# A two-layer hybrid attention kernel: five chunks of 512 columns in place of seven of 256 and 384

## The chip, the cores and the metric

The kernel runs on one core of one Trainium2 chip. The metric is the device time of one execution in microseconds; the times shown are the median of three runs and their spread. One further execution was recorded by the hardware profiler, and all rows below come from that one.

## The reference

There are two layers over 256 tokens with a model width of 1024, all in float32. In each layer the input is normed and multiplied by `w_in` (1024 x 3584) into ten groups of columns: queries, keys, values and gate of a block attention (`aq ak av ag`, 6 heads of 64, so 384 columns each), the same four of a dilated attention (`bq bk bv bg`, 384 each), and queries and gate of an attention over 256 rows of memory (`mq mg`, 4 heads, 256 each). Memory's keys and values come from the normed memory times `w_mem_kv` (1024 x 512). Queries and keys are normed per head and, but for memory's, rotated by position.

```python
a_q, a_k, a_v, a_g, b_q, b_k, b_v, b_g, m_q, m_g = jnp.split(proj, cuts, axis=-1)
qa = rope(rms_norm(to_heads(a_q, N_HEADS_MOBA), qk_g[0]))
mkv = jnp.einsum('bmd,de->bme', rms_norm(mem, mem_norm_g), w_mem_kv)
km = rms_norm(to_heads(m_k, N_HEADS_MEM), qk_g[5])
y = jnp.concatenate([oa * jax.nn.silu(a_g), ob * jax.nn.silu(b_g), om * jax.nn.silu(m_g)], axis=-1)
return x + jnp.einsum('bte,ed->btd', y, w_out)
```

At 256 tokens the block attention is one causal block, and the three dilated patterns are one attention whose mask holds the logarithm of how many patterns allow a pair.

## The kernel before, in words

**Products.** Each float32 matrix product is made of three products of a rounded format: weights and inputs are split into a high and a low half (`hi`, `lo` in L430 and L431; `xmh`, `xml` in L183 and L186), and `products` (L146) issues high x high, low x high and high x low. Only the first two of memory's eight blocks of rows go through whole, in full float32 (`WHOLE`).

**Projections.** `project` (L216) computes one chunk of n columns for both halves of the tokens: two accumulator banks, eight blocks of 128 rows, three products, so 48 matmuls of n columns. `project_t` (L235) computes the gates transposed, with 256 columns to a matmul. The order of the chunks is `order` (L371): memory's keys and values (`mkv`, 512 columns), `mq` 256, `mg`, `bq`, `bk`, `bv` 384 each, the gate in two parts, `aq`, `ak`, `av` 384 each, the gate, and then the rows of `w_out` for the three attentions. There are four accumulator banks (`acc`), three work banks (`wk`) and one for the outputs of a pair of heads.

**Weights.** `loads` (L389) brings units of up to 1 MB into three raw buffers by DMA, nearly all on SP's queue (the very first unit on ScalarE's), each as soon as a raw buffer is free. `split` (L419) makes the high half on ScalarE and the low half on VectorE, four splits ahead of their use.

**Order.** Every TensorE instruction is kept in the order in which the program was written out (`pe`, L103). That order is made by a small planner: `clock` adds up the time of the matmuls, and the attention of a pair of heads is a generator whose steps (turn queries and keys, scores, turn the probabilities, outputs) come due some microseconds of that clock later (`D_NORM`, `D_QK`, ... in L32) and are put between two steps of the projection that is then under way (`poll`, L125). The other engines run in program order where `pin` (L90) says so, which is the case up to the end of the first layer's first projections; behind it, the instructions are ordered by priority, which is program order where nothing else is said. An accumulator tile takes a bank that is free when the compiler's scheduler comes to it.

**Norms.** `normed` (L257) squares an accumulator on ScalarE, sums by head on VectorE, takes a power on GpSimd, and multiplies by one table (memory) or by two for the rotation, four or six VectorE instructions in all. `start_heads` (L546) starts the pairs of heads of a group when the norms of its queries and keys are issued: for `b` behind `bk`, for `a` behind `ak`, all three pairs at once.

**Start of the first layer.** `gT` holds the gains of the input norms and comes by GpSimd's queue. Memory's keys and values are projected from the unnormed rows; the factors of its norm (`rmem`) come later from the squares of `mem_sb` (L561 to L567) and scale the evicted tile `kv` (L572). Memory's keys are normed behind memory's queries (L570 to L573).

## Time and profile before

| | |
|---|---|
| median of 3 runs | 295.46 us (295.03 to 296.15) |
| the profiled execution | 295.58 us |
| its span, first to last instruction | 293.8 us |
| mean granted TensorE clock | 1.000 |
| TensorE matmul busy | 285.1 us, 97% |
| VectorE busy | 204.5 us, 70% |
| ScalarE busy | 200.1 us, 68% |
| GpSimd busy | 56.0 us, 19% |
| DMA | 47.33 MB, mean 161 GB/s |

Busy times come from single instructions; those of TensorE overlap, so that a start-to-start spacing is read from the timeline. In the rows, L is the line of the kernel, `out<-in` are the program's names, a form such as `128x384` is partitions x elements, and what stands in brackets is the idle time of the engine before that row and what ended it.

### The profile page before, as it was taken

To read this page: it belongs to the slowest core of one execution; us is meant where nothing else is said; L and a number is where in the kernel's file an instruction comes from. 1 tells how busy PE (TensorE), PEld (TensorE's weight loads), DVE (VectorE), ACT (ScalarE), POOL (GpSimd) and SP (SyncE) were. 2 spreads that over 40 slices of the span, in tenths; PEclk is the share of its full clock that TensorE was granted. 3 is DMA by queue.
4 is the path that set the end of the run, shared out by engine and by line. 5 is a ranking of instruction groups with operands and counts; after the bars stand their busy time and mean duration, and the time that the engine had idled before them with its cause. 6 is when DMAs were issued, how large, how long until landed. Compare 5 with 4: busy or idle time off the path is not lost.

```text
span 293.8 us, 4977 instructions
## 1 busy us (share of the span) xinstructions
PE 285.1 (97%) x1810; PEld 250.2 (85%) x1810; DVE 204.5 (70%) x456; ACT 200.1 (68%) x445; POOL 56.0 (19%) x74
## 2 busy tenths in 40 slices
PE   7799999999999999999999999999999999999994
PEld 5489989698998999877788999989899899987773
DVE  1588899887656997654485668879655699765413
ACT  2799968795888646987364654868588864698600
POOL 1003598030001230000011049703000123000000
PEclk9999999999999999999999999999999999999999
DMA  7999656327347248246207726560823715820003
GB/s 231 378 366 355 208 143 229 78 102 220 106 113 240 62 158 310 98 166 207 80 8 243 222 101 174 189 172 9 274 60 108 240 47 170 304 99 29 3 0 143
DMA packets 32681, 47.33 MB, mean 161 GB/s; under 512 B 1152, under 2 KB 27536, under 8 KB 32656
## 3 DMA queue, kind: packets, MB, share of 16 engines
q1 hardware_dynamic: 32048, 45.95, 48.4%
q10 hardware_dynamic: 576, 1.05, 1.0%
q8 instruction: 14, 0.23, 0.3%
q14 instruction: 11, 0.09, 0.1%
q0 software_dynamic: 32, 0.02, 0.0%
HBM read 45.96 MB, written 1.05 MB: 160 GB/s over the span
## 4 chain that ended last, share of the span: by engine, by line
PE 81%; DVE 6%; DMA 5%; ACT 3%; issue 2%; POOL 1%; SPq 0%; DVEq 0%; ACTq 0%
PE acc L111 64%; PE wk L114 7%; PE o L111 5%; PE wk L111 5%; DMA raw<-in_w_in_dram 3%; DMA memT<-in_mem_t_dram 2%; DVE lo L431 2%; DVE xml L186 1%; ACT hi L430 1%; POOL hrs L156 1%; DVE hss L263 1%; ACT xmh L183 1%; POOL r L156 0%; DVE ms L155 0%; ACT pr L334 0%
## 5 line engine op out<-in xcount | busy, mean ns | idle before, releaser
L431 DVE TENSOR_TENSOR lo<-raw,hi 128x768 fp32r<-128x768 f32 (+1 forms) x91 | 97.2, 1091 | 31.0 <-ACT hi L430 30.9
L430 ACT CAST hi<-raw 128x768 fp32r<-128x768 f32 (+1 forms) x91 | 83.8, 937 | 33.0 <-PE acc L111 24.4
L111 PE MATMUL acc<-hi,xmh 128*128 128x384 f32 (+2 forms) x252 | 67.0, 348 | 1.7 <-ACT hi L430 1.7
L111 PE MATMUL acc<-hi,xml 128*128 128x384 f32 (+2 forms) x252 | 63.6, 335 | 0.0
L111 PE MATMUL acc<-lo,xmh 128*128 128x384 f32 (+2 forms) x252 | 63.5, 335 | 0.0
L156 POOL TENSOR_TENSOR hrs<-ms,mhalf 128x6 f32<-128x6 f32 (+1 forms) x24 | 30.3, 1264 | 118.9 <-DVE ms L155 118.5
L111 PEld LDWEIGHTS acc<-hi,xmh 128*128 128x128 f32 x252 | 42.6, 189 | 7.1 <-issue 3.0
L111 PEld LDWEIGHTS acc<-lo,xmh 128*128 128x128 f32 x252 | 45.0, 188 | 1.2
L111 PEld LDWEIGHTS acc<-hi,xml 128*128 128x128 f32 x252 | 44.9, 188 | 1.2
L111 PE MATMUL acc<-hi,yT 128*128 128x512 f32 x128 | 41.0, 402 | 0.0
L111 PE MATMUL acc<-xmh,hi 128*128 128x256 f32 x128 | 29.7, 293 | 0.0
L341 ACT ACTIVATE pr<-pr,nm 128x128 f32<-128x128 f32 (+1 forms) x48 | 21.4, 446 | 12.0 <-DVE nm L339 11.8
L111 PE MATMUL acc<-xmh,lo 128*128 128x256 f32 x128 | 28.4, 283 | 0.0
L111 PE MATMUL acc<-xml,hi 128*128 128x256 f32 x128 | 28.3, 282 | 0.0
L111 PEld LDWEIGHTS acc<-hi,yT 128*128 128x128 f32 x128 | 23.0, 188 | 4.9 <-issue 0.7
L347 ACT ACTIVATE pr<-pr,rinv 128x128 f32<-128x128 f32 (+1 forms) x64 | 25.6, 462 | 0.0
L111 PE MATMUL acc<-lo,yT 128*128 128x512 f32 x64 | 25.0, 391 | 0.0
L111 PEld LDWEIGHTS acc<-xmh,hi 128*128 128x128 f32 x128 | 20.9, 191 | 0.7 <-issue 0.7
L111 PEld LDWEIGHTS acc<-xml,hi 128*128 128x128 f32 x128 | 21.0, 191 | 0.0
L111 PEld LDWEIGHTS acc<-xmh,lo 128*128 128x128 f32 x128 | 21.0, 191 | 0.0
L358 ACT COPY pT<-wk 128x384 f32<-128x384 f32 (+1 forms) x32 | 15.5, 506 | 6.8 <-PE wk L114 6.8
L339 DVE CUSTOM_DVE_ANT_0 pr<-wk,cst 128x128 f32<-128x128 f32 (+1 forms) x48 | 14.3, 354 | 5.3 <-PE wk L111 5.3
(77 smaller groups left out, 356.8 us busy)
## 6 DMA issues: line engine op xcount, KB each, us to landing
raw<-in_w_in_dram SPq DMA_DIRECT2D x24, 768.0 KB, 4.9
raw<-in_w_in_dram SPq DMA_DIRECT2D x7, 1024.0 KB, 5.3
raw<-in_w_out_dram SPq DMA_DIRECT2D x6, 1024.0 KB, 6.1
raw<-in_w_in_dram SPq DMA_DIRECT2D x6, 512.0 KB, 3.7
raw<-in_w_out_dram SPq DMA_DIRECT2D x4, 512.0 KB, 4.3
raw<-in_w_mem_kv_dram SPq DMA_DIRECT2D x2, 1024.0 KB, 5.2
raw<-in_w_mem_kv_dram ACTq DMA_DIRECT2D x4, 256.0 KB, 5.4
raw<-in_w_mem_kv_dram SPq DMA_DIRECT2D x2, 512.0 KB, 7.5
```

The source lines that it names most:

```text
L111: pe(nc.tensor.matmul(out, a, b, start=start, stop=stop), us)
L114: pe(nc.tensor.transpose(out, a, ident), 0.109)
L156: pin(nc.gpsimd.tensor_tensor(dst, ms, mhalf[:, :n], op=ALU.pow))
L183: pin(nc.scalar.activation(hi[:, k], v[:, a], AF.Copy, scale=g[:, k:k + 1]))
L186: pin(nc.vector.scalar_tensor_tensor(lo[:, k], v[:, a], g[:, k:k + 1], hi[:, k].bitcast(F32), op0=ALU.mult, op1=ALU.subtract))
L263: pin(nc.vector.tensor_reduce(ss, heads(sq), axis=AX.X, op=ALU.add))
L339: nc.vector.tensor_tensor_reduce(out=pr[:, spans[t]], in0=s[:, spans[t]], in1=masks[t], scale=-1.0, scalar=3e38, op0=ALU.add, op1=ALU.min, ...
L341: nc.scalar.activation(pr[:, spans[t]], pr[:, spans[t]], AF.Exp, scale=-1.0, bias=nm[:, t:t + 1], accum_out=sums[:, t:t + 1])
L347: nc.scalar.activation(pr[:, spans[t]], pr[:, spans[t]], AF.Copy, scale=rinv[:, t:t + 1])
L358: nc.scalar.copy(pT[:, :n], ps[:, :n])
L430: pin(nc.scalar.copy(hi, raw))
L431: pin(nc.vector.tensor_tensor(lo, raw, hi.bitcast(F32), op=ALU.subtract))
```

## The change

Queries, keys and values of a layer are projected in five chunks of 512 columns, put together from pieces of the column groups:

| chunk | columns |
|---|---|
| c0 | all of `mq`, `bv` 128 to 384 |
| c1 | all of `bq`, `bk` 0 to 128 (one piece in memory) |
| c2 | `bk` 128 to 384, `aq` 0 to 128, `bv` 0 to 128 |
| c3 | `aq` 128 to 384, `ak` 0 to 256 (one piece) |
| c4 | `ak` 256 to 384, all of `av` (one piece) |

The gate chunks and `w_out` stay. A unit of a mixed chunk is loaded with one DMA for each piece. `normed` is divided into `inverse_norms` (square, sum, power) and `normed` (the tables), which takes ranges of columns with a table for each. Queries and keys of a group share a tile `qk` of 768 columns.

Pairs of heads start in parts: the first pair of `b` behind c1, the other two behind c2; the first two of `a` behind c3, the last behind c4. `D_NORM` goes from 8 to 11. The norms, the softmax, the copies of turned tiles and the output products are issued with a priority 60 instructions earlier (`urgent`). In the first layer the squares of memory's rows, the scalings of `kv` and the norm of memory's keys are issued inside c0, and the constants' DMA earlier; the norm of memory's queries follows c0. The second layer's split of memory (`next_mem`) is started with `a` instead of `b`. `gT` is loaded on SP's queue behind the first block of memory, the fourth piece of the first weight unit on SP's queue, and `mem_sb` shares the buffer of the first weight unit.

```diff
-D_NORM, D_MEM, D_QK, D_SOFTMAX, D_PT, D_EVAC = 8, 1, 2.5, 5, 2.5, 4
+D_NORM, D_MEM, D_QK, D_SOFTMAX, D_PT, D_EVAC = 11, 1, 2.5, 5, 2.5, 4
+URGENT = 60
...
-    tc.keep_in_program_order(nc.gpsimd.dma_start(gT, gains))
...
+    def urgent():
+        return tc.high_priority(offset=URGENT)
...
+    def inverse_norms(acc):
+        n = acc.shape[-1]
+        with urgent():
+            sq = sp.tile([P, n], F32, tag="sq", name="sq", bufs=2)
+            pin(nc.scalar.activation(sq, acc, AF.Square))
...
+            rsqrt(rs, ss, n // HD, 1.0 / HD)
+        return rs
+    def normed(acc, rs, dst, tables):
+        n = acc.shape[-1]
+        with urgent():
+            t1 = sp.tile([P, n], F32, tag="t1", name="t1", bufs=2)
+            for lo, hi, tab in tables:
+                pin(nc.vector.tensor_tensor(heads(t1[:, lo:hi]), heads(acc[:, lo:hi]),
+                                            tab[0][:, None, :].to_broadcast([P, (hi - lo) // HD, HD]), op=ALU.mult))
...
-            step = 1 if u == 0 else 2 if u == 1 else 4 if u == 2 else nk
+            step = 1 if u == 0 else 2 if u == 1 else nk
...
-                queue = nc.scalar if u == 0 else nc.sync
+                queue = nc.scalar if u == 0 and b < 3 else nc.sync
...
+        if k == 0:
+            pin(nc.sync.dma_start(gT, gains))
...
-        mq, steps = project(xs, weights(), 256)
+        mq, steps = project(xs, weights(), 512)
...
-            if i == 3 and l == 0:
-                mem_junk = sp.tile([P, D], F32, tag="v", name="mem_junk", bufs=2)
+            if i == 1 and l == 0:
+                mem_junk = sp.tile([P, D], F32, tag="tab", name="mem_junk", bufs=1)
                 r_mem.append(row_scale(mem_sb, 0, "rmem", mem_junk))
+                pin(nc.sync.dma_start(cst, const))
+                load_gains(0, 4)
+            if i == 2 and l == 0:
+                r_mem.append(row_scale(mem_sb, 1, "rmem", mem_junk))
+                pin(nc.scalar.activation(kv[:, 0], kv[:, 0], AF.Copy, scale=r_mem[0]))
+            if i == 3:
+                if l == 0:
+                    pin(nc.scalar.activation(kv[:, 1], kv[:, 1], AF.Copy, scale=r_mem[1]))
+                for t in range(NT):
+                    normed(kn[:, t], inverse_norms(kn[:, t]), kn[:, t], [(0, 256, [gB[:, l, 5]])])
         for t, acc in enumerate(mq):
-            normed(acc, 256, qn[:, t], [gB[:, l, 4]])
...
+            normed(acc[:, 0:256], inverse_norms(acc[:, 0:256]), qn[:, t], [(0, 256, [gB[:, l, 4]])])
+            pin(nc.scalar.copy(v_b[:, t, 128:384], acc[:, 256:512]))
...
-            if l + 1 < DEPTH and kind == 2:
+            if l + 1 < DEPTH and kind == 0:
...
+                for t, acc in enumerate(run(project(xs, weights(), 512))):
+                    normed(acc, inverse_norms(acc), qk[:, t, 0:512], [(0, 384, table(2, t)), (384, 512, table(3, t))])
+                start_heads(range(1), e0, qn, kn, masks, v, gate, ready)
+                for t, acc in enumerate(run(project(xs, weights(), 512))):
+                    rs = inverse_norms(acc[:, 0:384])
+                    normed(acc[:, 0:256], rs[:, 0:4], qk[:, t, 512:768], [(0, 256, table(3, t))])
+                    nc.scalar.copy(v[:, t, 0:128], acc[:, 384:512])
+                    normed(acc[:, 256:384], rs[:, 4:6], qk_a[:, t, 0:128], [(0, 128, table(0, t))])
+                start_heads(range(1, 3), e0, qn, kn, masks, v, gate, ready)
```

## Rows read from the trace of the kernel before

**Rows 1.** The page's part 1: busy us, share of the span, instructions.

```profile
PE 285.1 (97%) x1810; PEld 250.2 (85%) x1810; DVE 204.5 (70%) x456; ACT 200.1 (68%) x445; POOL 56.0 (19%) x74
```

**Rows 2.** The waits of TensorE, longest first: us in total, times, longest us.

```profile
PE acc L111 <- ACT hi L430: 1.7, 1, 1.7
```

**Rows 3.** Timeline of TensorE: start us, us, what, count, idle before and its releaser.

```profile
1.04 3.35 PE L121 MATMUL warm<-blank 128*128 128x128 f32 x14 [1.04 <-DVE mhalf L83]
...
10.97 1.20 PE L111 MATMUL acc<-hi,xmh 128*128 128x512 f32 x4 [1.72 <-ACT hi L430]
...
13.84 1.07 PE L111 MATMUL acc<-hi,xmh 128*128 128x512 f32 x4
14.74 1.07 PE L111 MATMUL acc<-hi,xml 128*128 128x512 f32 x4
...
21.07 0.40 PE L111 MATMUL acc<-hi,xmh 128*128 128x256 f32 x2
...
32.34 0.40 PE L111 MATMUL acc<-xmh,lo 128*128 128x256 f32 x2
...
38.73 0.33 PE L114 MATMUL wk<-ident,kn 128*128 128x128 f32 x1 [0.46 <-DVE kn L277]
...
52.02 0.70 PE L111 MATMUL wk<-qkT 64*128 64x256 f32 x2
53.19 1.13 PE L111 MATMUL wk<-qkT 64*128 64x256 f32 x6 [0.48 <-ACT pT L358]
54.25 0.62 PE L111 MATMUL acc<-hi,xmh 128*128 128x384 f32 x2
```

**Rows 4.** The chain that ended last, in order of time: start us, us, what.

```profile
19.07 8.12 DMA raw<-in_w_in_dram
...
60.94 0.87 PE wk L114 x8
61.82 4.17 PE acc L111 x24
...
193.09 1.06 PE wk L111 x8
```

**Rows 5.** Groups of instructions by shape: busy us, mean ns of one, idle before.

```profile
L431 DVE TENSOR_TENSOR lo<-raw,hi 128x1024 fp32r<-128x1024 f32 x43 | 51.6, 1219 | 14.4 <-ACT hi L430 14.4
...
L431 DVE TENSOR_TENSOR lo<-raw,hi 128x768 fp32r<-128x768 f32 x48 | 45.8, 976 | 16.6 <-ACT hi L430 16.5
...
L532 DVE SCALAR_TENSOR_TENSOR gate<-th,acc 128x256 f32<-128x256 f32 x16 | 6.2, 415 | 4.1 <-ACT th L531 3.9
...
L531 ACT ACTIVATE th<-acc 128x256 f32<-128x256 f32 x16 | 5.4, 375 | 0.6 <-PE acc L111 0.6
```

**Rows 6.** Timeline of ScalarE, 22 to 30 us.

```profile
22.61 2.04 ACT L430 CAST hi<-raw 128x1024 fp32r<-128x1024 f32 x2
...
25.46 1.13 ACT L161 ACTIVATE mem_junk<-mem_sb 128x1024 f32<-128x1024 f32 x1
...
27.26 0.83 ACT L430 CAST hi<-raw 128x768 fp32r<-128x768 f32 x1 [0.58 <-DMA raw<-in_w_in_dram]
...
29.58 0.72 ACT L572 ACTIVATE v<-v,rmem 128x512 f32<-128x512 f32 x1
```

**Rows 7.** Two stretches: busy us of PE, PEld, DVE, ACT, POOL; clock, DMA, GB/s.

```profile
14.00:21.00 7.00, 7.00 (x40) 6.01 (x40) 5.63 (x12) 6.16 (x11) 1.13 (x2) 1.00 1.09 360
60.00:70.00 10.00, 10.00 (x72) 9.19 (x71) 10.00 (x19) 8.10 (x14) 2.65 (x2) 1.00 0.29 78
```

**Rows 8.** Timeline of VectorE, 29 to 32 us.

```profile
29.01 0.41 DVE L263 TENSOR_REDUCE hss<-sq 128x4 f32<-128x256 f32 x1
...
31.10 0.41 DVE L263 TENSOR_REDUCE hss<-sq 128x4 f32<-128x256 f32 x1
...
31.62 0.42 DVE L267 TENSOR_TENSOR t<-acc,gB 128x256 f32<-128x256 f32 x1
```

**Rows 9.** Timeline of GpSimd, 29 to 31 us.

```profile
29.70 1.02 POOL L156 TENSOR_TENSOR hrs<-ms,mhalf 128x4 f32<-128x4 f32 x1 [2.05 <-DVE ms L155]
```

More of the change, by code (lines that the diff above doesn't have):

```diff
@@ L287, in pair_of_heads @@
         qkT = sp.tile([P, 2, T], F32, tag="qkT", name="qkT", bufs=SLOTS)
-        nc.scalar.copy(qkT.rearrange("p c t -> p (c t)"), ps)
+        with urgent():
+            nc.scalar.copy(qkT.rearrange("p c t -> p (c t)"), ps)
         me = live["pairs"]
@@ L321, in pair_of_heads @@
         y = sp.tile([P, T], F32, tag="y", name="y", bufs=2)
-        nc.vector.scalar_tensor_tensor(y, o, 0.5, gate[:, pair], op0=ALU.mult, op1=ALU.mult)
+        with urgent():
+            nc.vector.scalar_tensor_tensor(y, o, 0.5, gate[:, pair], op0=ALU.mult, op1=ALU.mult)
         live["o"] -= 1
@@ L372, in hybrid_kernel @@
     for l in range(DEPTH):
-        order += [(l, c) for c in ["mkv", "mq", "mg", "bq", "bk", "bv", "bg0", "bg1", "aq", "ak", "av", "ag0", "ag1", "om", "ob", "oa"]]
+        order += [(l, c) for c in ["mkv", "c0", "mg", "c1", "c2", "bg0", "bg1", "c3", "c4", "ag0", "ag1", "om", "ob", "oa"]]
     units = []
@@ L379, in hybrid_kernel @@
         else:
-            n = 512 if c == "mkv" else in_cols[c][1]
+            n = 512 if c == "mkv" else sum(hi - lo for lo, hi in in_cols[c])
             nk = 8 if n <= 256 else 4
@@ L464, in hybrid_kernel @@
     load(RAW_BUFS + 1)
+    mem_sb = sp.tile([P, NT, D], F32, tag="yT0", name="mem_sb", bufs=1)
     pin(nc.sync.dma_start(mem_sb, mem.rearrange("(t p) c -> p t c", p=P)))
@@ L542, in finished @@
             done.add(e)
-            nc.scalar.copy(yT[0][:, e], y)
-            nc.vector.tensor_tensor(yT[1][:, e], y, yT[0][:, e].bitcast(F32), op=ALU.subtract)
+            with urgent():
+                nc.scalar.copy(yT[0][:, e], y)
+                nc.vector.tensor_tensor(yT[1][:, e], y, yT[0][:, e].bitcast(F32), op=ALU.subtract)
         def start_heads(pairs, e0, qn, kn, masks, v, gate, ready, delay=D_NORM):
-            for pair in range(pairs):
+            for i, pair in enumerate(pairs):
                 spawn(pair_of_heads(qn, kn, pair, masks, v, gate, ready,
-                                    lambda y, e=e0 + pair: finished(y, e)), delay + D_PAIR * pair)
-        qn, kn, kv, gate = head_tiles(256, 512)
-        v = kv[:, :, 256:512]
+                                    lambda y, e=e0 + pair: finished(y, e)), delay + D_PAIR * i)
+        kv, gate = head_tiles(512, 256)
+        kn, v = kv[:, :, 0:256], kv[:, :, 256:512]
+        qn = sp.tile([P, NT, 256], F32, tag="mqn", name="mqn", bufs=1)
+        v_b, gate_b = head_tiles(384, 384)
         ready = dict(gate=1e9)
-        mq, steps = project(xs, weights(), 256)
+        mq, steps = project(xs, weights(), 512)
         for i, _ in enumerate(steps):
@@ L584, in hybrid_kernel @@
                 masks = [cst[:, C_CAUSAL + 128:C_CAUSAL + 256], cst[:, C_CAUSAL:C_CAUSAL + 256]]
-            if l + 1 < DEPTH and kind == 2:
+            if l + 1 < DEPTH and kind == 0:
                 mem_xs = xm_tiles()
                 spawn(next_mem(mem_xs, gT[:, 24 + 8 * l:32 + 8 * l]), D_FIRST_MEM)
-            qn, kn, v, gate = head_tiles(384, 384)
             ready = dict(v=1e9, gate=1e9)
-            for i, dst in ((0, qn), (1, kn)):
-                for t, acc in enumerate(run(project(xs, weights(), 384))):
-                    normed(acc, 384, dst[:, t], (tab[:, kind + i, 0, t], tab[:, kind + i, 1, t]))
@@ L593, in hybrid_kernel @@
-            start_heads(3, e0, qn, kn, masks, v, gate, ready)
-            for t, acc in enumerate(run(project(xs, weights(), 384))):
-                nc.scalar.copy(v[:, t], acc)
+            if kind == 2:
+                v, gate, qk, qk_a = v_b, gate_b, queries_and_keys(), queries_and_keys()
+                qn, kn = qk[:, :, 0:384], qk[:, :, 384:768]
+                for t, acc in enumerate(run(project(xs, weights(), 512))):
[7 more added lines that the diff above has]
+                start_heads(range(1, 3), e0, qn, kn, masks, v, gate, ready)
+            else:
+                (v, gate), qk = head_tiles(384, 384), qk_a
+                qn, kn = qk[:, :, 0:384], qk[:, :, 384:768]
+                for t, acc in enumerate(run(project(xs, weights(), 512))):
+                    normed(acc, inverse_norms(acc), qk[:, t, 128:640],
+                           [(0, 256, table(0, t)), (256, 512, table(1, t))])
+                start_heads(range(2), e0, qn, kn, masks, v, gate, ready)
+                for t, acc in enumerate(run(project(xs, weights(), 512))):
+                    normed(acc[:, 0:128], inverse_norms(acc[:, 0:128]), qk[:, t, 640:768], [(0, 128, table(1, t))])
+                    nc.scalar.copy(v[:, t], acc[:, 128:512])
+                start_heads(range(2, 3), e0, qn, kn, masks, v, gate, ready)
```

121 lines of the change are left out of this document (55 added, 66 removed), and 4 rows, old and new, of the table in_cols.

## The prediction

> **What bounds the kernel now.** I read the busy shares first. TensorE's matmul row is busy 97% of the span, VectorE 70% [rows 1]. A busy matmul row only says that some matmul was in flight, so the next view is the list of waits with TensorE alone: its largest entry is one wait of 1.7 us near the start [rows 2]. Then the timeline, to see at what spacing the matmuls start, since durations overlap. Matmuls over 512 columns start four per 0.90 us (13.84 to 14.74), 226.7 ns each to the precision of a longer run; those over 256 columns are 48 + 48 from 21.07 to 32.34, 94 spacings of 119.9 ns [rows 3]. Over 384 columns the chain of waits shows a pure run of 24 in 4.17 us, 173.6 ns [rows 4]. So the middle of the kernel is one stream of matmuls back to back, and a matmul costs its columns over 2.4 GHz plus about 13.3 ns: 106.7 + 13.2, 160 + 13.6, 213.3 + 13.4. The reader is to see two things: the stream has hardly a hole outside the start, and its price per matmul is known at all three widths.
>
> The holes that are left lie in the first layer. At 38.73 TensorE has waited 0.46 us for normed memory keys. At 52.02 the scores of the second memory pair begin, stop after two of eight matmuls, and the next matmul of a projection comes at 54.25: 2.23 us [rows 3] where eight such matmuls take 1.06 us elsewhere [rows 4], so 1.17 us lost behind a ScalarE copy that frees a work bank.
>
> **The change part by part.** *Five chunks of 512.* Per layer the queries', keys' and values' projections were 48 matmuls of 256 columns and 6 x 48 of 384: 48 x 119.9 + 288 x 173.6 = 5.76 + 50.00 = 55.75 us. Now they are 5 x 48 of 512: 240 x 226.7 = 54.41 us. The columns are the same 122,880; what goes is the fixed part of 96 matmuls, 1.3 us a layer, **2.6 us** for both. It lies on the stream that sets the end, so it counts in full.
>
> The Trainium skill, "TensorE: Matmul & The Clock Gate", section "Back-to-back issue gap", speaks against this part: there the isolated spacing at the full clock is the columns over 2.4 GHz plus 2.5 ns. By that, 96 matmuls fewer are worth 0.24 us a layer and 0.5 us in all. This trace doesn't agree: the remainder is 13 ns at each of three widths [rows 3, 4], and the sum keeps 2.6 us.
>
> *Splits and norms.* Per layer, 2 splits of 1024 and 24 of 768 elements become 20 of 1024: on VectorE 20 x 1.219 against 2 x 1.219 + 24 x 0.976, 1.5 us less [rows 5]. The norms go the other way: 64 VectorE instructions a layer become 80, since a chunk that holds queries and keys multiplies by two tables. From the two split sizes an instruction's fixed part is at most 0.25 us, so up to 4 us more. Off the path while the stream's weights are split a chunk ahead; if that cover went, it would be paid in the windows after the two big norms, where VectorE is already full (below). Moving the next layer's memory split to the second group empties ScalarE and VectorE in the first layer's busiest stretch.
>
> *TensorE later behind a norm (8 to 11 us), norms and softmax ahead of later work.* The waits at 38.73 and 52.02 go: the memory pairs are turned at 12 us behind the first chunk instead of 9, and the copy that blocked the scores now ranks ahead of the splits beside it. Gain 0 to 1.6 us; I take **1.6**, since both waits were for work that stood behind splits.
>
> *Gains vector and the fourth weight piece move to SP's queue.* The first matmuls wait for a gain vector, but what follows waits for the memory block and the weights' high half until 10.97 [rows 3], so only that restart counts. One quarter of the first weight leaves ScalarE's queue and goes behind that block: between 0 and 0.8 us earlier, and then the second half of the normed input, which nothing here hurries, holds the stream again. I take 0.2 us. The extra DMAs (two to three for each unit of a mixed chunk) are issues on SP, which waits for buffers most of the time.
>
> *Memory's keys normed inside the first chunk.* This is the step that can cost. In the first layer all of it is pinned in program order. After the first chunk's second step ScalarE must take, in this order: the high half of the memory gate's weights, the square of memory row 0, the second high half, the square of row 1, the scaling of the values' first half, the high half of the next chunk, the second scaling; only then the squares of the keys, and behind them those of the queries. The first of these waits for its DMA. Before, that transfer (768 KB) ran from 19.07 to 27.19 [rows 4], and ScalarE waited for it [rows 6]. Now it is 1 MB; at about 360 GB/s [rows 7] 256 KB more are 0.7 us: 27.9. Then three high halves at 1.0, two squares at 1.1, two scalings at 0.65 [rows 6]: 6.5 us, and the first keys' square is done at about 34.8. VectorE does four norms in strict order, 2.09 us each (reduction at 29.01, the next at 31.10) because each waits for a power on GpSimd of 1.02 [rows 8, 9]; before, the queries came first, now the keys. The queries' banks are read for the last time 0.94 us into the third and the fourth norm (31.62 + 0.42 - 31.10): 34.8 + 4.2 + 0.9 = 39.9 and 42.0.
>
> TensorE's side: the first chunk starts at 21.07 and takes 48 x 0.2267 = 10.9 us, the memory gate 48 x 0.12 = 5.8: it reaches the next chunk at 37.7. There are four accumulator banks; two hold the queries, two the memory gate. The new chunk needs two at once. The gate's banks come free after a tanh of 0.38 and a product of 0.42 each [rows 5], some 38.6 and 39.3, if VectorE lets the products in between its norms. So the stall is 1.6 us with the gate's banks, 2.2 with one of each, 4.3 with the queries' two, and nothing only if ScalarE is not held as I reckon. Queued behind the waiting matmul is all of TensorE's order. I take **2.2**, the middle case. In the second layer nothing waits for memory's rows, and the keys are normed half a chunk before the queries.
>
> **Sum**, on the profiled execution (295.58 us, span 293.8 and 1.8 around it; 0.12 above the median of the runs): -2.6 - 1.6 - 0.2 + 2.2 = -2.2 us. On the median of 295.46 that is **293.3 us**.
>
> **The rivals.** *The stall at the second chunk is not there* (ScalarE reaches the norms earlier, or the gate's banks come free at once): -2.6 - 1.6 - 0.2 = -4.4, 291.1 us. For it: before, the queries' norm was off the path. Against it: ScalarE did wait for that DMA, and the order is fixed.
>
> *The stall is whole*: the new chunk gets the queries' own banks and waits for the fourth norm. -4.4 + 4.3: 295.4 us, no change. For it: before, in this place the new chunk did follow the queries' banks and found them read (31.62 + 0.42) just half a microsecond before it began. Against it: with the keys first, the gate's banks are free sooner.
>
> *Slower: the whole stall and then a slow clock.* The granted clock is 1.00 in every stretch shown [rows 7], but the 14 warm-up matmuls, the first after idleness, ran at 0.22 us apiece (13 spacings in 3.35 less one duration of 0.42) [rows 3], where 128-column transposes take 0.109 (0.87 for eight) [rows 4]: half the rate, the 1.2 GHz level. The Trainium skill, "TensorE: Matmul & The Clock Gate", in its table "Why this matters for your kernels", warns of idle gaps between bursts of matmuls for this reason; no gap in this trace behind the warm-up is long enough to show it. If TensorE idles some 4 us and restarts at half rate for as long as the warm-up lasted, it loses half of 3.4 us or, over twice that time, 3.4: -4.4 + 4.3 + 1.7 to 3.4 = +1.6 to +3.3, 297.1 to 298.8 us. It decides from a stall at which the granted clock falls below 1.00; with one bank free in the middle of the wait a matmul breaks the gap, which speaks against it.
>
> **How the numbers follow.** Half a per cent is 1.5 us, about what this kernel's runs (295.03 to 296.15) can tell from none. Chances: the middle stall 0.43 (its own range 292.3 to 294.6), no stall 0.22, the whole stall 0.22, slower 0.13, into which I also put VectorE falling behind: it is busy 10.00 of 10 us in 60 to 70 [rows 7], there without holding TensorE. Faster by over 0.5% (under 294.0): all of no stall and about four fifths of the middle, 0.56. Slower by over 0.5% (over 296.9): 0.13. Within: 0.31. The range leaves out a tenth at each end: 291.0, just under no stall, to 296.6, between the whole stall and the slow clock.
>
> **What would show it.** Right: 240 matmuls of 512 columns a layer 0.227 us apart; no wait at the memory pairs' scores; TensorE's longest wait, 1.5 to 2.5 us, before the first matmul of the chunk behind the memory gate at about 38 us, released by VectorE; ScalarE waiting for the gate's weights until about 28. Wrong: a spacing at 512 columns clearly above 0.227 us, a gap over 1 us in the second layer, a granted clock under 1.00, or waits of TensorE for low halves behind the norms of the 512-column chunks, which would mean that VectorE has become the bound.

## The result and the profile after

The changed kernel takes **308.27 us** (median of 4 runs, 307.18 to 309.68) against 295.68 on the same chip: 1.0435 times as long, 95% interval 1.0408 to 1.0462. The forecast was 293.3 us, in a range of 291.0 to 296.6; the kernel is 12.6 us slower than before and far outside the range.

The page of the changed kernel, part 1 and two rows of part 2 (40 slices of 7.7 us), stands against [rows 1]:

```profile
PE 289.6 (94%) x1618; PEld 230.4 (75%) x1618; DVE 205.4 (67%) x476; ACT 199.4 (65%) x437; POOL 56.1 (18%) x73
...
PE   8999849999899999989999999999989999989994
...
PEclk9999968999999999999999999999999999999999
```

192 matmuls fewer, and VectorE and ScalarE as busy as before in microseconds. No engine got work that would explain 12 us, so TensorE must stand still or run slower. Part 2 shows both: slices at 8 or less, and a clock row that dips in the sixth and seventh slice. The list of TensorE's waits (us in total, times, longest) names what it stands for; before, the longest wait was 1.7 us [rows 2]:

```profile
PE acc L114 <- DVE ms L158: 5.3, 1, 5.3
PE wk L117 <- ACT pr L363: 2.4, 4, 0.7
PE wk L117 <- DVE nm L355: 2.4, 2, 1.2
...
PE wk L117 <- ACT pT L375: 0.7, 2, 0.4
...
```

**The wait ahead of the second chunk.** TensorE's timeline of the changed kernel at its start and at the first matmul of c1 (start, us, then the row's name; in brackets the idle time before and what ended it), against [rows 3]:

```profile
10.03 1.20 PE L114 MATMUL acc<-hi,xmh 128*128 128x512 f32 x4 [0.58 <-ACT hi L451]
...
36.62 0.40 PE L114 MATMUL acc<-xmh,lo 128*128 128x256 f32 x2
42.36 1.51 PE L114 MATMUL acc<-hi,xmh 128*128 128x512 f32 x2 [5.34 <-DVE ms L158]
43.66 1.05 PE L114 MATMUL acc<-hi,xml 128*128 128x512 f32 x2
...
47.08 1.01 PE L114 MATMUL acc<-lo,xmh 128*128 128x512 f32 x2
...
48.39 0.62 PE L114 MATMUL acc<-hi,xml 128*128 128x512 f32 x2
...
49.75 0.62 PE L114 MATMUL acc<-hi,xml 128*128 128x512 f32 x2
```

5.34 us without a matmul, and behind it pairs of matmuls 0.86 us apart (43.66 to 47.08: 3.42 for eight) instead of 0.453 (48.39 to 49.75: 1.36 for six). The windows of the changed kernel (stretch, its us, busy us of PE, PEld, DVE, ACT and POOL, then the granted clock, the DMA share and GB/s) give half the clock, the 1.2 GHz level, over 41 to 48 us.

```profile
36.00:41.00 5.00, 1.02 (x9) 0.81 (x7) 4.06 (x10) 4.58 (x8) 2.24 (x2) 1.00 0.53 149
41.00:48.00 7.00, 5.64 (x13) 4.16 (x14) 5.74 (x14) 1.34 (x3) 2.37 (x3) 0.51 0.74 219
48.00:55.00 7.00, 7.00 (x35) 5.79 (x34) 3.38 (x4) 3.22 (x5) 6.88 (x16) 1.00 0.48 152
```

Why 5.34? The list names `ms`, which ended last before the restart (at 42.29), but VectorE's product for the gate (`gate`, done at 42.21) is what frees a bank. ScalarE first, to compare with [rows 6], then VectorE over the wait, to compare with [rows 8], both of the changed kernel:

```profile
29.12 1.05 ACT L451 CAST hi<-raw 128x1024 fp32r<-128x1024 f32 x1 [3.45 <-DMA raw<-in_w_in_dram]
...
35.29 0.71 ACT L265 ACTIVATE sq<-v 128x256 f32<-128x256 f32 x2
...
37.12 0.63 ACT L555 ACTIVATE th<-acc 128x256 f32<-128x256 f32 x2
...
42.65 0.37 ACT L607 COPY v<-acc 128x256 f32<-128x256 f32 x1 [2.07 <-DVE t L278]
```

```profile
38.13 0.41 DVE L267 TENSOR_REDUCE hss<-sq 128x4 f32<-128x256 f32 x1
38.46 1.22 DVE L452 TENSOR_TENSOR lo<-raw,hi 128x1024 fp32r<-128x1024 f32 x1
...
40.00 1.22 DVE L452 TENSOR_TENSOR lo<-raw,hi 128x1024 fp32r<-128x1024 f32 x1
41.14 0.41 DVE L289 TENSOR_TENSOR v<-t,hrs 128x256 f32<-128x256 f32 x1
41.47 0.41 DVE L267 TENSOR_REDUCE hss<-sq 128x4 f32<-128x256 f32 x1
41.80 0.41 DVE L556 SCALAR_TENSOR_TENSOR gate<-th,acc 128x256 f32<-128x256 f32 x1
```

c1 got one bank of memory's gate and the queries' first one. The gate's tanh is done at 37.75 (37.12 + 0.63), but the product that frees its bank starts at 41.80: VectorE takes it in its order behind the second norm of memory's keys and two low halves of c1's own weights, which are needed only once c1 runs. The queries' bank costs another 0.49 us: c1's second matmul, at 43.07, waits for ScalarE's copy of the values out of that bank (42.65 to 43.02), and not for the gate's second product. The size of the wait is that of one execution: in the profiles of the runs 3, 8, 11 and 12 below, whose program is the same up to here, it was 3.9 to 5.0 us.

**Late attention, in both layers.** To turn a tile is to transpose it by a product with the unit matrix (`wk<-ident`); the softmax of a pair of `a` or `b` begins when VectorE adds the masks to its scores (`pr<-wk,cst`). The first pair of `b` and the last of `a` show it, in TensorE's and VectorE's timeline of the changed kernel:

```profile
75.66 1.02 PE L114 MATMUL wk<-qkT 64*128 64x128 f32 x8
...
83.84 0.84 PE L117 MATMUL wk<-ident,pr 128*128 128x128 f32 x3 [0.73 <-ACT pr L363]
...
129.04 0.93 PE L114 MATMUL wk<-qkT 64*128 64x128 f32 x8
130.31 0.66 PE L117 MATMUL wk<-ident,qk 128*128 128x128 f32 x4 [0.34 <-ACT pT L375]
132.15 0.55 PE L117 MATMUL wk<-ident,pr 128*128 128x128 f32 x3 [1.18 <-DVE nm L355]
```

```profile
73.37 0.42 DVE L278 TENSOR_TENSOR t<-acc,tab 128x256 f32<-128x256 f32 x1 [2.29 <-ACT sq L265]
...
80.67 0.43 DVE L289 TENSOR_TENSOR qk<-t,hrs 128x256 f32<-128x256 f32 x1 [0.82 <-POOL hrs L159]
...
81.22 0.28 DVE L355 CUSTOM_DVE_ANT_0 pr<-wk,cst 128x128 f32<-128x128 f32 x1
...
128.97 2.36 DVE L452 TENSOR_TENSOR lo<-raw,hi 128x1024 fp32r<-128x1024 f32 x2 [0.45 <-ACT hi L451]
131.25 0.28 DVE L355 CUSTOM_DVE_ANT_0 pr<-wk,cst 128x128 f32<-128x128 f32 x1
```

The scores begin at 75.66; VectorE reads them first at 81.22, 5.6 us later, when c2's norms (73.37 to 81.1) are through, and TensorE stands at 83 for the probabilities. The last pair of `a` has its queries turned at 130.31 between another pair's scores and its softmax, on the third work bank, while the masks stand behind two low halves. Against the usual spacing of each kind of matmul these holes (64, 82.8, 129.6, 207, 226, 273) sum to some 7.6 us, good to half a microsecond.

**The account** on the profiled executions (308.51 against 295.58, +12.9): wait ahead of c1 5.3 + 0.5; half clock 2.7 (first experiment); late attention 7.6; against it the packing 2.6, the two old waits 1.6, the start 0.9 (10.97 to 10.03). That is +11.0, and 1.9 us are left. Most of them, 1.6 us, are three smaller delays in each layer behind the same probabilities (0.2 to 0.3 us each, at 84.2 to 85.5 and 227.7 to 228.9). The start is no gain of its own: what TensorE is early, it waits longer ahead of c1. In the third run it restarts at 10.72, and that wait is 3.9 us.

### The profile page after: what moved, and what is told of

Read it like the earlier page. It is cut to its first block, busy times and chain, and to the rows that moved or that the text cites. A ratio compares the mean times of both kernels' runs of the same rounds, so it can differ in the third digit from the quotient of the medians.

```text
span 306.7 us, 4622 instructions
## 1 busy us (share of the span) xinstructions
PE 289.6 (94%) x1618; PEld 230.4 (75%) x1618; DVE 205.4 (67%) x476; ACT 199.4 (65%) x437; POOL 56.1 (18%) x73
## 4 chain that ended last, share of the span: by engine, by line
PE 59%; ACT 15%; DVE 11%; DMA 7%; issue 5%; POOL 2%; POOLq 0%; SPq 0%; DVEq 0%; ACTq 0%
PE acc L114 48%; PE wk L117 5%; DVE lo L452 4%; DMA raw<-in_w_in_dram 3%; ACT pr L363 3%; ACT hi L451 3%; PE o L114 3%; ACT pr L357 2%; PE wk L114 2%; DMA x_sb<-in_x_dram 2%; ACT pr L350 2%; POOL hrs L159 2%; DVE t L278 1%; DVE hss L267 1%; DMA raw<-in_w_mem_kv_dram 1%
## 5 line engine op out<-in xcount | busy, mean ns | idle before, releaser
L452 DVE TENSOR_TENSOR lo<-raw,hi 128x1024 fp32r<-128x1024 f32 x79 | 96.1, 1226 | 44.9 <-ACT hi L451 44.9
L451 ACT CAST hi<-raw 128x1024 fp32r<-128x1024 f32 x79 | 81.9, 1050 | 43.6 <-PE acc L114 31.3
L114 PE MATMUL acc<-hi,xmh 128*128 128x512 f32 x188 | 61.7, 415 | 5.9 <-DVE ms L158 5.3
L114 PE MATMUL acc<-hi,xml 128*128 128x512 f32 x188 | 58.1, 397 | 0.0
L114 PE MATMUL acc<-lo,xmh 128*128 128x512 f32 x188 | 57.8, 395 | 0.0
L159 POOL TENSOR_TENSOR hrs<-ms,mhalf 128x4 f32<-128x4 f32 (+3 forms) x24 | 31.2, 1300 | 140.5 <-DVE ms L158 140.5
L114 PEld LDWEIGHTS acc<-hi,xmh 128*128 128x128 f32 x188 | 33.2, 192 | 14.0 <-issue 7.5
L363 ACT ACTIVATE pr<-pr,rinv 128x256 f32<-128x256 f32 (+1 forms) x64 | 25.1, 462 | 0.0
L117 PE MATMUL wk<-ident,pr 128*128 128x128 f32 x104 | 18.1, 284 | 5.4 <-ACT pr L363 2.4
L117 PEld LDWEIGHTS wk<-ident,pr 128*128 128x128 f32 x104 | 11.9, 140 | 12.8 <-ACT pr L363 5.8
```

The costliest lines, as they stand in the source:

```text
L114: pe(nc.tensor.matmul(out, a, b, start=start, stop=stop), us)
L117: pe(nc.tensor.transpose(out, a, ident), 0.109)
L159: pin(nc.gpsimd.tensor_tensor(dst, ms, mhalf[:, :n], op=ALU.pow))
L363: nc.scalar.activation(pr[:, spans[t]], pr[:, spans[t]], AF.Copy, scale=rinv[:, t:t + 1])
L451: pin(nc.scalar.copy(hi, raw))
L452: pin(nc.vector.tensor_tensor(lo, raw, hi.bitcast(F32), op=ALU.subtract))
```

## The experiments

All are edits of the changed kernel (of 308.27 us); ratios are to the kernel before.

**1. Keep TensorE at work during the wait.** 26 products of the unit matrix go between the gate and c1 in the first layer.

```
+        if l == 0:
+            filler = o_p.tile([P, T], F32, tag="o", name="filler")
+            for _ in range(26):
+                pe(nc.tensor.matmul(filler[:, 0:P], ident, ident, start=True, stop=True), 0)
```

> The changed kernel with 26 idle matmuls of 128 columns (52 records of 0.109 us, 5.7 us) put on TensorE between the first layer's memory gate and the next chunk, where it stands still for 5.5 us. Theory A (the stand-still lets the granted clock fall to half, and half a clock from 41.1 to 47.9 us costs the matmuls of 42.4 to 47.9 half of that time, 2.8 us): the clock stays 1.00, the next chunk still begins at 42.4 to 42.6, and the kernel takes 305.3 us, 2.8 less than the changed one's 308.3. Rival (the low clock costs nothing, since the chunk's weights or norms are late anyway): same time, 308.3, or more by up to 0.2.

305.57 us, 1.035 [1.031, 1.039]. A window of this kernel shows the clock at its full level in the same place:

```profile
41.00:48.00 7.00, 7.00 (x39) 6.01 (x38) 5.42 (x10) 2.54 (x5) 3.70 (x5) 1.00 0.73 231
```

The stretch in which TensorE stood is filled, c1 begins as late as before (42.11), and the time came as expected. So the half clock costs 2.7 us, which the two intervals leave open by some 1.4; the late attention stayed as it was.

**2 to 5. Memory's part moved, the last pair of `a` earlier.** The second squares memory's first row at the first step of c0 and puts its second row, the scalings and the keys' norm back behind the queries' norm, in both layers; the third starts the last pair of `a` 3 us earlier (`D_NORM - 3`); the fourth does both; the fifth squares and scales both rows of memory at the first step of c0 and norms the keys behind the queries, in the first layer alone:

```
+            if i == 0 and l == 0:
...
+                for t in range(NT):
+                    r_mem.append(row_scale(mem_sb, t, "rmem", mem_junk))
+                for t in range(NT):
+                    pin(nc.scalar.activation(kv[:, t], kv[:, t], AF.Copy, scale=r_mem[t]))
```

The keys' norm behind the queries' (second and fifth) and the earlier pair (third):

```
-            if i == 3:
...
-                for t in range(NT):
-                    normed(kn[:, t], inverse_norms(kn[:, t]), kn[:, t], [(0, 256, [gB[:, l, 5]])])
...
+        for t in range(NT):
...
+            normed(kn[:, t], inverse_norms(kn[:, t]), kn[:, t], [(0, 256, [gB[:, l, 5]])])
...
-                start_heads(range(2, 3), e0, qn, kn, masks, v, gate, ready)
+                start_heads(range(2, 3), e0, qn, kn, masks, v, gate, ready, D_NORM - 3)
```

> The changed kernel with memory's part of the first chunk put back: the square of row 0 ahead of the gate's weights, the square of row 1, the scalings and the norm of memory's keys behind the norm of the queries, in both layers. TensorE's order is unchanged. Theory A (the products that free the gate's banks, and the queries' reads, stand behind the keys' norms on VectorE, and these behind a DMA): the queries' banks are read by about 36.3 us, TensorE's wait at 36.9 goes, the clock stays 1.00, and 5.5 + 2.8 us go: 300.0 us. Rival (VectorE has too much to do in that stretch, whatever its order): the wait moves or stays above 3 us, 304 us or more.

> The changed kernel with the last pair of the block attention turned 3 us of the planner's clock earlier (8 us behind the last chunk instead of 11), in both layers. Theory A (that turn takes the third work bank between the scores of the pair before and the turn of the probabilities, which then waits until VectorE has read a score bank: 0.7 + 1.35 us a layer at 130 and 274 us): both waits go, 4.1 us less, 304.2 us. Rival (the probabilities or the masks are late because VectorE has two splits ahead of them): the waits stay in size and change their releaser, 307 to 308 us.

> The two edits of the runs on memory's order and on the early pair together. Theory A: the gains add, 308.3 - 8.3 - 4.1 = 295.9 us, level with the kernel before; left are the waits of 0.7 to 1.0 us for probabilities behind the norms of the two big chunks. Rival: they overlap, since a kernel without the first wait is 8 us earlier with the same due times, and 298 us or more are left.

> The changed kernel with another order in the first layer only: memory's rows are squared and its keys and values scaled right behind their eviction, while ScalarE would wait for the gate's weights (3.5 us idle there), and memory's keys are normed behind the queries. TensorE's order is unchanged. Theory A (the stand-still is the queue of VectorE behind the keys' norms, and the keys' lateness in the run with memory's old order was the squares of row 1 standing behind the queries): queries' banks are read by 36 us, the keys are ready by 42, neither wait comes, the clock stays 1.00, and the time is that of the changed kernel less 5.5 + 0.8 + 2.8: 299.2 us. Rival (VectorE's work of that stretch is too much in any order): one of the two waits stays above 1.5 us and the clock falls, 303 us or more.

305.45 (1.032 [1.030, 1.035]), 305.33 (1.032 [1.029, 1.035]), 304.14 (1.029 [1.026, 1.031]) and 304.47 (1.029 [1.025, 1.033]): each gains, none as much as its removed wait. The third takes most of what it aimed at (2.06 to 0.49 in each layer). In the others the rival's number came. The second and fifth move the wait: the keys now come behind the queries and are late at their turn (2.08 and 1.88 us). In the profiled execution of each the clock fell to half behind it; three other executions of the second had a mean clock of 1.000 and took 304.79 to 305.49 us, so this is not what holds the gain down. TensorE's timeline and a window of the second:

```profile
38.69 0.50 PE L114 MATMUL acc<-hi,xmh 128*128 128x512 f32 x1 [1.33 <-DVE gate L556]
...
49.37 0.30 PE L117 MATMUL wk<-ident,v 128*128 128x128 f32 x1 [2.08 <-DVE v L289]
```

```profile
50.00:54.00 4.00, 4.00 (x14) 3.21 (x13) 0.00 (x0) 0.88 (x2) 3.92 (x15) 0.57 0.77 264
```

In this place four norms and the splits of two chunks come at once; in these orders a bank or memory's keys are late, whichever goes first. Here the list puts c1's wait (1.33) down to the gate's product itself.

**6. Without the priority.**

```
-URGENT = 60
+URGENT = 0
```

> The changed kernel with the priority offset 0 instead of 60; TensorE's order is the same. Theory A (the waits for probabilities come from due times that are too early for the norms of 512 columns, not from the priorities; the offset helps them a little): the waits at 64, 83, 207 and 226 us grow by 0.3 to 1.5 us each, 309 to 314 us. Rival (the offset lets norms pass the softmax and the splits, and makes these waits): they shrink, 305 to 307 us.

314.12 us, 1.065 [1.061, 1.070]. The priority is worth 5.9 us here, near theory A's number but not for its reason: the waits for probabilities shrank from 2.4 to 0.9 us, as the rival had it, and the outputs of the memory pair wait for `y` behind splits (3.3 us in each layer). The mean clock fell too, from 0.989 to 0.978, so part of the 5.9 us is half clock.

**7, 8. Probabilities turned 1 us later,** with the edits of 3 and 5, and alone.

```
-D_NORM, D_MEM, D_QK, D_SOFTMAX, D_PT, D_EVAC = 11, 1, 2.5, 5, 2.5, 4
+D_NORM, D_MEM, D_QK, D_SOFTMAX, D_PT, D_EVAC = 11, 1, 2.5, 6, 2.5, 4
```

> The order of the run with memory's rows early, the last block pair 3 us earlier, and the planner's time for a softmax 6 us instead of 5, in the changed kernel. Theory A (the three account for the loss: 9.1, 3.1 and 3.2 us): 308.3 - 15.4 = 292.9 us, 3 us faster than before, which is the saving of the 512-column matmuls. Rival (later due times push attention into the next stretch and the end of the layer, where TensorE then waits for the outputs): 295 to 298 us.

> The changed kernel with the planner's time for a softmax 6 us instead of 5. Theory A (probabilities come 0.7 to 0.9 us later than the planner has them, four times): these four waits go, 3.2 us less, 305.1 us. Rival (the waits move with the due time, since VectorE is what is behind): 307 to 308.5 us.

300.55 (1.016 [1.012, 1.019]) and 304.43 (1.031 [1.028, 1.034]). The seventh gained half of the 15.4 us that were added up for it, and neither number came: left are waits for the probabilities of the first pair of `b` (1.92 and 1.72) and for memory's keys (1.07). Alone, the later turn takes away two of the four waits that it aimed at (64 and 207) and most of those at 130 and 273, at which it did not aim. The other two, for probabilities behind c2, stay: 1.18 + 0.58 us where there were 0.9. So the eighth came near its number partly by luck.

**9 to 12. Due times.** The first pair of `b` 15 us and 8.5 us behind c1 instead of 11, on top of the seventh, with the memory pairs moved too (9, 10); `D_NORM` 8 instead of 11 (11); the pairs of a group together as in the kernel before (12, all of `b` behind c2, and likewise `a` behind c4):

```
-                start_heads(range(1), e0, qn, kn, masks, v, gate, ready)
+                start_heads(range(1), e0, qn, kn, masks, v, gate, ready, 15)
...
-D_NORM, D_MEM, D_QK, D_SOFTMAX, D_PT, D_EVAC = 11, 1, 2.5, 5, 2.5, 4
+D_NORM, D_MEM, D_QK, D_SOFTMAX, D_PT, D_EVAC = 8, 1, 2.5, 5, 2.5, 4
...
-                start_heads(range(1), e0, qn, kn, masks, v, gate, ready)
...
-                start_heads(range(1, 3), e0, qn, kn, masks, v, gate, ready)
+                start_heads(range(3), e0, qn, kn, masks, v, gate, ready)
```

> On top of the three edits (memory's rows squared at once in the first layer, last pair of a 3 us earlier, softmax delay 6), the first pair of b is turned 15 us behind c1 instead of 11, so that its scores fall behind the norms of c2, and the memory pairs of the first layer are turned 2.5 us later, so that memory's keys are normed by then. Theory A (a softmax that comes due while VectorE and ScalarE norm a 512-column chunk is late, and TensorE waits at the turn of its probabilities): against the kernel with the three edits (300.55, profiled 298.66) four waits go: 1.07 at the turn of memory's keys, 0.65 at 70, 1.92 at 78, 1.72 at 220, together 5.4 us: 293.5 to 295.5. Rival (the norms only push the lateness on to what is due next, since both engines are too full there): waits of the same size come back at the second and third pair of b, 299 to 301.

> As the kernel with the three edits, but the first pair of b is turned 8.5 us behind c1, so that its softmax is issued before the norms of c2 come, and the memory pairs in the second layer are turned 9 us behind c0, before the norms of c1. Theory A: the waits at the probabilities of the first pair of b (1.92 and 1.72) and of the memory pair (0.65) go, but the turn of the queries comes about 0.5 us behind the end of c1's norm, so up to 1 us of a new wait a layer: 294.5 to 297. Rival (lateness is pushed on): 299 to 301.

> The changed kernel with D_NORM 8 as before instead of 11, nothing else. Theory A (the delay moved work out of the reach of norms, as it was meant, and a norm of a 512-column chunk takes about 8 us): turned queries and keys are late at the turns, 1 to 3 us more in each layer at the first pair of b and the memory pair: 309 to 313. Rival (the longer delay itself moved scores and softmax into the next chunk's norms): the waits at the probabilities shrink, 302 to 306.

> The changed kernel, but the pairs of a group start together as in the kernel before: all of b behind c2, all of a behind c4. Theory A (attention ahead of later parts puts a softmax beside the norms of the next chunk): the waits of 0.9 in each layer behind c2 and of 2.06 in each layer at the turn of the last pair of a go, 5.9 us: 302 to 303.5. Rival (without the early pairs the attention is late at the end of the layer, where w_out waits for its outputs): 306 to 312, with waits at om, ob or oa.

304.57 (1.031 [1.027, 1.034]), 307.99 (1.042 [1.036, 1.048]), 308.86 (1.045 [1.041, 1.048]) and 320.42 (1.082 [1.077, 1.087]). In the ninth, tenth and twelfth the rival had the direction, and each went further than its numbers: lateness is pushed on, to the memory pair's probabilities (2.3 us) and a gate (3.6) in the ninth, the probabilities of `b` (4.8 us in six waits) in the tenth. In the eleventh neither number came: the time is the same, the waits are others (turned queries and keys 2.4 us in all, probabilities 3.0). The twelfth is the dearest: with the last keys of `a` in c4, only the gate is left to hide all three pairs, and `w_out` waits for them. Its TensorE timeline, in c4 where `b`'s probabilities are late, and ahead of `w_out`:

```profile
107.82 0.33 PE L117 MATMUL wk<-ident,pr 128*128 128x128 f32 x1 [1.85 <-ACT pr L363]
...
148.63 0.50 PE L114 MATMUL acc<-hi,yT 128*128 128x512 f32 x1 [2.08 <-ACT yT L571]
```

So starting the pairs in parts is worth 12 us to this packing, a part of it through the clock (a mean of 0.968 to 0.983 against 0.980 to 0.993), and it is what puts a softmax beside norms.

**13 to 16. Volume or order?** Without the rotation (the products with the second table and the addition are left out); the softmax ahead of the norms; that with the seventh's edits and the gates urgent; the seventh with the rotation's addition on GpSimd.

```
-            if len(tables[0][2]) > 1:
+            if False:
...
     def head(me, s, spans, masks, pTs):
 
-        with urgent():
+        with urgent(400):
...
-                pin(nc.vector.tensor_tensor(t1, t1, t2, op=ALU.add))
+                pin(nc.gpsimd.tensor_tensor(t1, t1, t2, op=ALU.add))
```

> The changed kernel without the rotation in the norms (the product with the second table and the addition are left out, so its output is not the reference's): 24 products and 16 additions a layer fewer on VectorE, some 16 us of its 205, in the stretches behind c1 to c4; the order of TensorE is the same. Theory A (VectorE's volume behind the wide norms makes the attention late): of the late waits of 7.6 us at most 2.5 are left, the first layer's wait of 5.5 us and its half clock stay: 301 to 303. Theory B (priority: the norms go ahead of the softmax that is due): a norm is a third shorter, so a third of the lateness goes: 305 to 306.5. Theory C (ScalarE or the work banks, not VectorE): no change, 307.5 to 309.

> The changed kernel with the softmax of a pair issued 400 instructions earlier in priority instead of 60, so that it goes ahead of the norms; the order of TensorE is the same. Theory B: the waits of 0.7 to 0.9 us for probabilities behind c1 and c2 go in both layers, about 3.5 us, and the norms have 3 us of slack by D_NORM 11: 304 to 305.5. Theory A (too much volume): what is late changes, not how late; waits come at the turns of queries and keys or at the splits: 307 to 310.

> The kernel with three edits (rows squared at once, last pair of a earlier, softmax delay 6; 300.55, profiled 298.66) and the softmax ahead of the norms, and the gates with the priority of the norms. Theory B: its waits of 1.92 and 1.72 at the first pair of b and of 0.65 at the memory pair go; what is left is about 2 us ahead of c1 and at memory's keys: 295 to 297. Theory A: 299 to 302.

> The kernel with three edits, with the addition of the two halves of a rotation on GpSimd instead of VectorE (16 a layer, 5.3 + 2.3 us and the narrower ones, some 9 us of VectorE in all); the order of TensorE is the same. Theory A: VectorE is free earlier by 0.3 to 1.4 us behind each chunk, the waits at the first pair of b shrink by that: 297 to 299. Rival: GpSimd takes longer for an addition than VectorE (its power over 8 columns takes 1.0 us), the normed queries and keys come later and TensorE waits at their turn: 301 to 305.

313.80 (1.060 [1.057, 1.063]): with less to do on VectorE the kernel is slower still (1.060 against 1.0435), which no theory had. VectorE and TensorE of that kernel behind c2:

```profile
77.83 0.43 DVE L289 TENSOR_TENSOR qk<-t,hrs 128x256 f32<-128x256 f32 x1 [1.11 <-POOL hrs L159]
...
80.61 0.63 DVE L289 TENSOR_TENSOR qk<-t,hrs 128x256 f32<-128x256 f32 x2 [1.01 <-POOL hrs L159]
81.15 0.28 DVE L355 CUSTOM_DVE_ANT_0 pr<-wk,cst 128x128 f32<-128x128 f32 x1
```

```profile
76.05 0.92 PE L114 MATMUL wk<-qkT 64*128 64x128 f32 x6 [1.38 <-ACT pT L375]
...
84.94 0.33 PE L117 MATMUL wk<-ident,pr 128*128 128x128 f32 x1 [1.56 <-ACT pr L363]
```

VectorE idles 1.11 and 1.01 us for GpSimd's powers with the masks ready behind them, and takes them at 81.15, as the changed kernel does (81.22). In this stretch the chain of a norm (ScalarE, VectorE, GpSimd, VectorE) sets the pace, not the sum of its work. VectorE is busy 14 us less (191.2), and yet the waits for probabilities grew from 2.4 to 4.5 us. So volume alone is not what makes the attention late. The smaller volume also came in a new order, and no run parts the two.

Another part of the 5.5 us is the clock. The clock row of that kernel's page dips three times, in the sixth, twelfth and thirty-first slice, the last two behind these waits and their twins in the second layer:

```profile
PEclk9999959999979999999999999999998999999999
```

Its mean is 0.978 over 312.2 us, against 0.989 over 306.7: by that, up to 3.5 us of full speed more are lost (an estimate).

303.86 (1.028 [1.022, 1.033]) for the softmax first. VectorE of that kernel takes the masks in the middle of c2's norms:

```profile
72.57 0.54 DVE L267 TENSOR_REDUCE hss<-sq 128x6 f32<-128x384 f32 x1
...
74.56 0.28 DVE L355 CUSTOM_DVE_ANT_0 pr<-wk,cst 128x128 f32<-128x128 f32 x1
...
78.89 0.54 DVE L267 TENSOR_REDUCE hss<-sq 128x6 f32<-128x384 f32 x1
```

All four waits for probabilities are gone; a bank wait of 0.84 came in each layer, so the late attention is 5.8 us instead of 7.6. The time is near what was expected, but only partly for this reason: the wait ahead of c1 happened to be 0.9 us shorter, which is within its spread, and the clock there 0.77 over 41 to 48 instead of 0.51. The fifteenth is as the seventh (300.52, 1.015 [1.011, 1.019]): the probabilities' waits went, and the norm that had to stand back is late at its own turn (1.54 and 1.36 us). GpSimd's addition (308.29, 1.042 [1.038, 1.045]) goes the rival's way and beyond its numbers: it takes 1320 ns over 512 columns, where VectorE took 693, in the chain that paces the norm. (The power over eight columns takes 1.65 us there, not 1.0.) TensorE waited elsewhere than the rival had it, for a work bank at the turn of probabilities (2.27 us in each layer) and not at the turn of queries and keys; how the longer addition leads there is not shown. Its row in the groups of that kernel, and VectorE's in those of the changed kernel (busy us, mean ns):

```profile
L288 POOL TENSOR_TENSOR t<-t,t 128x512 f32<-128x512 f32 x8 | 10.6, 1320 | 0.0
```

```profile
L288 DVE TENSOR_TENSOR t<-t,t 128x512 f32<-128x512 f32 x8 | 5.3, 693 | 0.0
```

**17, 18. All remedies, due times fitted.** The fifteenth with softmax delay 5, the first pair of `b` at 13 us and the first layer's memory pairs 1.5 us later; then (18, the last two lines) that pair at 17 in the first layer and the second memory pair's probabilities 2 us later.

```
+        start_heads(range(2), 6, qn, kn, None, v, gate, ready, D_NORM + D_MEM + (1.5 if l == 0 else 0))
...
+                start_heads(range(1), e0, qn, kn, masks, v, gate, ready, 13)
...
+                start_heads(range(1), e0, qn, kn, masks, v, gate, ready, 13 if l else 17)
...
+        yield D_SOFTMAX + D_HEAD * (me % 2) + (2 if me in (2, 3) else 0)
```

> The changed kernel with memory's rows squared at once in the first layer, the softmax ahead of the norms, the gates with the priority of the norms, the last pair of a 3 us earlier, the first pair of b 2 us later (13 us behind c1), and the memory pairs of the first layer 1.5 us later; softmax delay 5. Against the kernel with three edits and the softmax first (300.52; its profiled run 300.55, with holes of 0.75 before c1, 1.09 at memory's keys, 1.54 and 1.36 at the turn of the first pair of b, 0.80 before w_out). Theory B (order and due times are all of it): the two turns, the keys and the w_out wait go, 4.8 us: 295 to 297, no slower than the kernel before by more than 0.5%. Rival (with 512-column chunks each placing meets another norm): waits of 0.5 to 2 us elsewhere, 298 to 302.

> The kernel before this one (297.95; profiled 298.46), but in the first layer the first pair of b is turned 17 us behind c1 instead of 13, and the probabilities of the second memory pair are turned 2 us later. Theory B (order and due times are all of it): the hole of 3.3 us at 63 and the half clock behind it, some 1.7 us, go: 293 to 295, below the kernel before by what the packing saves. Rival (each placing meets another norm): TensorE waits 1.5 to 3 us at the turn of the probabilities that come next, 296 to 298.5.

**297.95** (1.007 [1.005, 1.010]) and 298.68 us (1.012 [1.009, 1.015]). The two can hardly be told apart. Neither reached theory B's numbers: 297.95 lies between its two forecasts, 298.68 just beyond the rival's. 10.3 of the 12.6 us are back, and the second layer has hardly a hole. In the first layer one large one is left, TensorE and a window of the seventeenth:

```profile
66.78 0.66 PE L117 MATMUL wk<-ident,qk 128*128 128x128 f32 x4 [3.16 <-ACT pr L350]
```

```profile
68.00:70.00 2.00, 2.00 (x7) 1.61 (x7) 0.00 (x0) 2.00 (x6) 0.00 (x0) 0.50 1.05 403
```

Moving that pair turned it into two others in the eighteenth, at outputs and at a gate's bank, where the rival had named the turn of probabilities:

```profile
67.63 1.08 PE L114 MATMUL o<-pT,v 128*64 128x256 f32 x6 [1.18 <-ACT pT L375]
...
82.81 0.50 PE L114 MATMUL acc<-hi,xmh 128*128 128x512 f32 x1 [2.26 <-DVE gate L557]
```

No version beat the kernel before. Whether one exists with this packing stays open.

## Why the prediction was wrong

**The five chunks: right.** 512 columns cost 0.2267 us each (1.36 us for six, 48.39 to 49.75), as in the sum, so 2.6 us are saved on the stream.

**Start and old waits: right in sign.** The two old waits are gone. The restart came 0.9 us earlier, not 0.2, but in one execution of each kernel: the profiles of the experiments, whose start is the same, have it at 8.7 to 10.7. And it gained nothing, since c1 waits for VectorE.

**Memory's keys ahead of the queries: right place and banks, wrong size.** The step "the gate's banks come free some 38.6 and 39.3, if VectorE lets the products in between its norms" failed, and with it the reads of the queries' first bank at 39.9. c1 did get one bank of each, the middle case. But VectorE did not let the products in: the gate's bank came free at 42.21, and the queries' at 43.02. ScalarE was 0.9 us late (the keys' squares run from 35.29 on, where the first was to be done at 34.8; the gate's weights at 29.12, not 27.9). The rest is two low halves in VectorE's order and the copy of the values, which the forecast left out. TensorE was at c1 at 37.0 and not 37.7. So the wait is 5.8 us instead of 2.2, and more than the bound of 4.3. The slow clock, which I had given 0.13, then came too: 2.7 us against 1.7 to 3.4 in that rival, which had the clock right; its 297.1 to 298.8 us lacked the late attention. The windows show the clock: 1.00 up to 41, and 0.51 from there to 48, in and behind the gap of 5.34 us. The Trainium skill, "TensorE: Matmul & The Clock Gate", in its table "Why this matters for your kernels", warns of idle gaps between bursts of matmuls; with that these windows agree.

**Norms and due times at nothing: the step that failed most.** "Off the path while the stream's weights are split a chunk ahead" looked only at splits. What was late was the softmax, some 7.6 us in both layers, and I had no term for it, nor for the pairs that start in parts. Before, the chunks of a group behind its keys (values, gate) have no norms, and scores at 71.25 are masked at 73.75; TensorE's and VectorE's timeline of the kernel before:

```profile
71.25 0.93 PE L111 MATMUL wk<-qkT 64*128 64x128 f32 x8
```

```profile
73.75 0.28 DVE L339 CUSTOM_DVE_ANT_0 pr<-wk,cst 128x128 f32<-128x128 f32 x1
```

With values packed beside keys, the next norm comes one chunk of 10.9 us later, its norms take some 8 us (73.37 to 81.1 for c2), and the planner puts the scores 2.5 us behind the turn: a pair turned 11 us behind its chunk has its scores behind the next chunk's norms in the order of issue, and one turned 8 us behind it finds its own norm unfinished. The eleventh run shows both sides at the same time (308.86 and 308.27), the fourteenth that order is what delays the probabilities behind c1 and c2, the thirteenth that less volume alone does not help. That the stretch is too tight for any order was not shown. Two of the forecast's signs of being wrong came true, a gap over 1 us in the second layer (1.18) and a clock under 1.00; the third did not, since none of TensorE's waits in the changed kernel is for a low half.

**The chances.** The forecast's stretch of VectorE at 10.00 of 10 us [rows 7] was put down to no harm since it held nothing up there. In hindsight it was a warning that order would decide once something due stood in it.

## What to carry to other kernels

Packing that lengthens a chunk removes little time by itself, here 1.3 us a layer; ask what ran in the chunk that it swallows, since a stretch without norms was where the softmax had been hidden. Price an engine's in-order work by what stands ahead of the one instruction that frees a bank, not by its busy share, and do it for every bank that the next matmul can get. A longer chain across engines can delay what stands behind it even where an engine in it idles, as VectorE did in the thirteenth.

## What the hardware showed unexpectedly

Less work on VectorE made the kernel slower (the thirteenth, 313.80 against 308.27), with its instructions in an order made anew and the clock at half in three places. And the clock: behind TensorE's gaps of 5.34 us (changed kernel), 3.16 (seventeenth) and 2.08 (second, on a stretch with other waits) the granted clock read 0.51, 0.50 and 0.57 in the windows shown. In the tenth it read 0.57 over 107 to 111, behind waits of 1.28 and 0.36 us. But the profiled execution of the eighteenth, with gaps of 1.18 and 2.26, had a mean clock of 1.000, while three of its other five had 0.994. So in these runs the length of a gap alone does not tell whether the clock falls.
